# Layer 1's features split four chunks at once, tables first, four row buffers in layer 0's output projection, the last latent's k on VectorE, C's conversions moved

## The chip, the core and the metric

The kernel runs on one core of a Trainium2 chip. The metric is the device time of one execution in microseconds (us). The core has a tensor engine (PE, with the loading of its weights listed apart as PEld), a vector engine (VectorE, DVE), a scalar engine (ScalarE, ACT), a GpSimd engine (POOL) and a synchronising engine (SyncE, SP), which here issues nearly all DMAs, in its program's order. Each engine runs its own list of instructions in order and waits for the others by semaphores.

## The reference

Two layers of a transformer trunk work on 512 latent tokens and 128 context tokens of width 1024. Each layer is

```
m = silu(cond) @ w_mod + b_mod ; shift, scale, gate = split(m, 3)
h = rmsnorm(x, g) * (1 + scale) + shift
... = split(h @ w_in)                       # queries, keys, values, gates of two mixers
y = concat(attend1 * silu(gate1), attend2 * silu(gate2)) @ w_out
x = x + gate * y
```

with one conditioning vector for the latents and one for the context. Layer 0 has the mixers A (latent attention: 8 heads, queries and keys are made by an up-projection from a compressed row, normalised per head, rotated in their last 32 columns) and B (a neighbourhood attention). Layer 1 has C (grouped-query attention, 8 query heads on 2 key heads, rotary) and D (windowed attention with a sink logit). Latent queries read latent and cached context keys in one softmax; context tokens read context alone. The outputs are x of both groups and the layers' new cache rows. All is float32.

## The kernel before

The 640 tokens are five tiles of 128 (tiles 0 to 3 latents, tile 4 context). Every matrix product in float32 accuracy is done in three passes over a high part and a low part of both operands (`PASS`): ScalarE writes the high part as a rounded copy, and VectorE or GpSimd the low part as the difference. Weights come in 128x512 pieces in the order in which they are needed: `load_raw` (L165) fetches a piece on SP's queue into one of four buffers `raw`; `conv` takes the next piece, `split_w` splits it into a tile W or Wc (L171 the high part on ScalarE, L172 the low part on VectorE for odd pieces and on GpSimd for even ones) and then asks for another raw piece.

The program is written stage by stage, and a scheduler of the framework, which plays the program through with its own costs, sets the order on each engine. `after(key, f)` lets what f issues come no earlier than the instruction kept in `hold[key]`. Matmuls that nothing urgent needs (gates, the next mixer's inputs) are units of a list `filler`; `fill(ns)` emits units up to a budget between steps of attention, so that TensorE has work while a softmax runs.

The change touches three stages.

The end of A's up-projection: `e_up(t)` makes A's queries Aq and keys Ak of a tile. `e_q_end` multiplies Aq by its norm's factor on VectorE (L1046) and rotates it; for the context tile t = 4 that is one multiplication by the cosines, on GpSimd (L1050). `e_k` scales the key, on GpSimd (L1026 and the line after it). After the last tile eight pieces of layer 0's output weights are split. Then `a_prep(0)` transposes Ak and Aq (L660) for the first head. At the same time the modulation of layer 1 is computed: `matvec` (L223) multiplies columns of w_mod, loaded into `wm` (L215), of which there are two buffers.

Layer 0's output projection, with layer 1's features and its product C1 behind it: `out_proj` multiplies each tile's result by the gate (L1286, from PSUM to `otmp`) and adds it to the old row `xres` (L1287), which is loaded by DMA (L1255) into one buffer of the pool ldp for t = 0, 2, 4 and one of p for t = 1, 3. `l1_norm` stores the row and normalises it to `xn`. `l1_h` transposes xn four 128-column chunks at a time into one PSUM bank, and `h_evac` applies scale and shift per chunk: the high part (L282, ScalarE), the float32 value (L287 on VectorE for even chunks, L285 on ScalarE for odd ones) and the low part (L288, GpSimd for even, VectorE for odd). `l1_c1` (L302, from `tok_units`) multiplies by C1's weights; `cpost` behind it rotates with the tables that `tables` makes (L1324) from the row `orow` (L814).

The start of mixer C: pieces of GC (C's gate weights) are split, `fill` emits gate matmuls (L325), `k_prep` prepares the keys, `q_prep` transposes and splits the first two query heads (L634, L640), and the scores (L1515, L1517) begin.

## Time and profile before

Three runs took 821.66, 822.66 and 824.35 us, median 822.66 us. The profiled execution took 823.33 us, of which the recorded span is 821.6 us; 1.7 us lie outside the span.

| Engine | busy us | share of the span | instructions |
|---|---|---|---|
| PE | 756.0 | 92% | 4533 |
| PEld | 621.3 | 76% | 4533 |
| DVE | 590.8 | 72% | 1448 |
| ACT | 466.4 | 57% | 1189 |
| POOL | 245.3 | 30% | 303 |

The mean granted clock of TensorE is 0.981. The chain that ended last is put down to PE for 61%, to DVE for 17%, to ACT for 10% and to DMA for 5%. The DMA engines moved 85.19 MB, 104 GB/s over the span. A share is a mean over the whole span; which engine holds up which is seen in the waits of one stretch.

### The profile page before, as it was taken

The page shows a single profiled execution, that of the slowest core. Times are in us where ns is not written, and L with a number is a line of the kernel's source. Part 1 is how long each engine was busy: PE and PEld are TensorE (multiplying, and loading weights), DVE is VectorE, ACT ScalarE, POOL GpSimd, SP SyncE. Part 2 cuts the span into 40 slices and gives each one's busy share as a digit, 9 for nine tenths or more (in the row PEclk, how much of TensorE's full clock was granted, in tenths as well). Part 3 has the DMA queues.
Part 4 walks back from the last instruction along what each step waited for, and adds up shares of the span by engine and source line. Part 5 has one row for each costly group of instructions (what it writes and reads, how often), then busy time and mean ns, then how long its engine had stood idle before and what let it go on. Part 6 is the DMA issues. An engine that isn't in the chain of part 4 may idle for free.

```text
span 821.6 us, 13182 instructions
## 1 busy us (share of the span) xinstructions
PE 756.0 (92%) x4533; PEld 621.3 (76%) x4533; DVE 590.8 (72%) x1448; ACT 466.4 (57%) x1189; POOL 245.3 (30%) x303
## 2 busy tenths in 40 slices
PE   4797899999999979999999899799989998899998
PEld 3496898988989857777676677796858796876776
DVE  5466958686766778676676978678689876666855
ACT  6437575766656666454464757575445556745610
POOL 0465526262343550111031135103143420422210
PEclk9898999999999989999999999899999999999999
DMA  9957122211252077434475611203030110332144
GB/s 302 333 139 213 27 67 57 54 54 35 68 173 78 1 248 214 117 88 117 130 214 147 230 37 41 85 1 103 1 109 30 65 40 1 119 61 39 27 132 151
DMA packets 80436, 85.19 MB, mean 104 GB/s; under 512 B 7617, under 2 KB 64577, under 8 KB 80321
## 3 DMA queue, kind: packets, MB, share of 16 engines
q1 hardware_dynamic: 77488, 79.10, 31.7%
q0 software_dynamic: 2880, 5.24, 4.1%
q8 instruction: 36, 0.59, 0.3%
q14 instruction: 32, 0.25, 0.1%
HBM read 72.97 MB, written 13.98 MB: 106 GB/s over the span
## 4 chain that ended last, share of the span: by engine, by line
PE 61%; DVE 17%; ACT 10%; DMA 5%; issue 4%; POOL 2%; SPq 0%; DVEq 0%; ACTq 0%; POOLq 0%
PE ps_t L302 13%; PE ps_t L325 9%; PE ps_t L1130 6%; PE ps_t L1231 6%; PE ps_t L588 4%; PE ps_t L484 3%; PE ps_t L562 3%; PE ps_t L223 3%; PE ps_s L1203 2%; DVE W L172 2%; PE ps_s L772 2%; DVE P L417 2%; ACT W L171 2%; PE ps_t L461 1%; ACT P L428 1%
## 5 line engine op out<-in xcount | busy, mean ns | idle before, releaser
L302 PE MATMUL ps_t<-W,hT 128*128 128x384 f32 (+2 forms) x735 | 162.4, 368 | 8.7 <-DVE gB L337 3.0
L302 PEld LDWEIGHTS ps_t<-W,hT 128*128 128x128 f32 x735 | 131.6, 191 | 20.4 <-DVE gB L337 3.3
L325 PE MATMUL ps_t<-hT,W 128*128 128x320 f32 x768 | 125.5, 317 | 5.1 <-DVE W L172 1.9
L325 PEld LDWEIGHTS ps_t<-hT,W 128*128 128x128 f32 x768 | 116.3, 192 | 8.2 <-DVE W L172 2.2
L172 POOL TENSOR_TENSOR W<-raw,W 128x512 fp32r<-128x512 f32 (+1 forms) x54 | 73.3, 1362 | 92.3 <-ACT W L171 89.7
L171 ACT ACTIVATE W<-raw 128x512 fp32r<-128x512 f32 (+1 forms) x106 | 62.9, 620 | 24.1 <-DMA raw<-in_w_in_even 11.0
L1130 PE MATMUL ps_t<-W,ytp 128*128 128x512 f32 x240 | 62.9, 405 | 3.0 <-ACT PT L370 1.6
L370 ACT ACTIVATE PT<-ps_t 128x512 f32<-128x512 f32 (+2 forms) x80 | 42.2, 527 | 40.2 <-PE ps_t L562 22.5
L368 DVE COPY PT<-ps_t 128x512 f32<-128x512 f32 (+2 forms) x80 | 48.2, 604 | 23.0 <-PE ps_t L562 13.4
L533 ACT ACTIVATE P<-ps_s,m 128x640 f32<-128x640 f32 x64 | 50.6, 792 | 24.2 <-DVE m L532 15.9
L172 DVE TENSOR_TENSOR W<-raw,W 128x512 fp32r<-128x512 f32 (+1 forms) x52 | 50.5, 976 | 17.5 <-ACT W L171 17.2
L532 DVE TENSOR_REDUCE m<-ps_s 128x1 f32<-128x640 f32 x64 | 51.9, 817 | 9.4 <-PE ps_s L1517 4.9
L1130 PEld LDWEIGHTS ps_t<-W,ytp 128*128 128x128 f32 x240 | 43.2, 188 | 15.8 <-ACT PT L370 2.6
L428 ACT ACTIVATE P<-P,m 128x384 f32<-128x384 f32 (+3 forms) x64 | 42.3, 663 | 10.7 <-DVE m L417 10.4
L288 POOL TENSOR_TENSOR hT<-h,hT 128x128 fp32r<-128x128 f32 (+1 forms) x34 | 24.3, 722 | 80.0 <-ACT hT L282 36.4
L1231 PE MATMUL ps_t<-W,yt 128*128 128x512 f32 (+1 forms) x207 | 47.7, 384 | 0.0
L1231 PEld LDWEIGHTS ps_t<-W,yt 128*128 128x128 f32 x207 | 37.1, 188 | 8.6 <-DVE gb L368 0.4
L562 PE MATMUL ps_t<-ident,P 128*128 128x128 f32 x256 | 39.1, 277 | 2.2 <-DVE rt L115 1.0
L562 PEld LDWEIGHTS ps_t<-ident,P 128*128 128x128 f32 x256 | 29.8, 140 | 13.6 <-issue 5.6
L1139 POOL DMA_DIRECT2D part<-part x20 | 17.5, 873 | 73.6 <-DVE part L1136 73.6
L536 DVE TENSOR_SCALAR P<-P,den 128x640 f32<-128x640 f32 x64 | 37.3, 584 | 1.8
L461 PE MATMUL ps_t<-ident,P 128*128 128x128 f32 x224 | 31.7, 276 | 5.2 <-DVE PT L368 1.7
(307 smaller groups left out, 1632.9 us busy)
## 6 DMA issues: line engine op xcount, KB each, us to landing
wm<-in_w_mod SPq DMA_DIRECT2D x16, 1024.0 KB, 8.6
raw<-in_w_in_odd SPq DMA_DIRECT2D x40, 256.0 KB, 2.9
raw<-in_w_in_even SPq DMA_DIRECT2D x36, 256.0 KB, 3.6
wm<-in_w_mod SPq DMA_DIRECT2D x16, 512.0 KB, 5.2
part<-part POOLq DMA_DIRECT2D x20, 256.0 KB, 4.7
xres<-part SPq DMA_DIRECT2D x10, 512.0 KB, 4.1
raw<-in_w_out_even SPq DMA_DIRECT2D x16, 256.0 KB, 3.3
raw<-in_w_out_odd SPq DMA_DIRECT2D x16, 256.0 KB, 3.0
```

The source lines that it names most:

```text
L171: S.activation(out=dst_hi, in_=src, func=AF.Copy)
L172: (V if i % 2 else G).tensor_tensor(out=dst_lo, in0=src, in1=f32(dst_hi), op=OP.subtract)
L302: T.matmul(ps[:, 0:c1 - c0], lhsT=hT[:, k, x, 128 * t:128 * t + 128], rhs=W[c, k][:, y, c0:c1], start=(k == 0 and i == 0), stop=(k == 7 an ...
L325: T.matmul(ps[:, 0:320], lhsT=W[c, k][:, x, c0:c0 + 128], rhs=hT[:, k, y, 320 * hf:320 * hf + 320], start=(k == 0 and i == 0), stop=(k == ...
L368: V.tensor_copy(out, in_)
L370: S.activation(out=out, in_=in_, func=AF.Copy)
L428: S.activation(out=P[:, e, 0:n], in_=src[:, e, 0:n], func=AF.Exp, scale=-1.0, bias=m[:, e:e + 1], accum_out=den[:, e:e + 1])
L532: V.tensor_reduce(out=m, in_=s[:, :, 0:320], axis=AX.XY, op=OP.min)
L533: S.activation(out=P.rearrange("p (u n) -> p u n", u=2), in_=s[:, :, 0:320], func=AF.Exp, scale=-1.0, bias=m, accum_out=den)
L562: T.transpose(ps[:, 128 * b:128 * b + 128], P[:, 128 * b:128 * b + 128], ident)
L1130: T.matmul(ps, lhsT=yts[l, t][:, i, x, :], rhs=W["WO%d%d" % (l, hf), k][:, y, :], start=(i == 0 and j == 0), stop=(i == 3 and j == 2))
L1231: T.matmul(ps, lhsT=yt[:, i - i0, u, :], rhs=W["WO%d%d" % (l, hf), k][:, v, c0:c1], start=(i == 0 and j == 0), stop=(i == 3 and j == 2))
```

## The change

Six things are changed.

1. `conv`: the low part of every GC piece is made by VectorE, not by turns.
2. `h_evac4` replaces `h_evac` in layer 1. It takes four chunks at once: for the first four the scale and shift are two VectorE instructions over 512 columns with broadcast operands, for the other four ScalarE still does each chunk; then one ScalarE copy makes the high part and one subtraction over 512 columns the low part (GpSimd for the first four, VectorE for the others). The float32 value goes into xn itself.
3. For t = 4 `e_k` and the cosine multiplication of `e_q_end` run on VectorE, `e_k` first. The eight splits of output weights behind them are issued after the last high part of head 0's `a_prep`.
4. `out_proj` of layer 0 has one row buffer in ldp (t = 0 and 4) and three in p (t = 1 to 3); the loads of t = 1 to 3 are issued at the start.
5. `l1_start` makes the sink row and the tables of tiles 0 and 1 at once; before, they stood behind the normalisation of tile 1.
6. Four GC pieces are split after the features of tile 3 and four after those of tile 4 (before, all eight after the last). At the start of C the first `q_prep` stands ahead of the last 1900 ns of filler, and the tables of tile 3 behind it.

```diff
@@ -198,7 +198,7 @@
         w = ns * n
         t = wtile()
         r = raws.pop(i)
-        split_w(t[:, 0, 0:w], t[:, 1, 0:w], r[:, 0:w], i if odd is None else odd)
+        split_w(t[:, 0, 0:w], t[:, 1, 0:w], r[:, 0:w], (1 if c == "GC" else i) if odd is None else odd)
         W[c, k] = t
         if i < 4:
             after("raw", load_raw)
@@ -286,6 +286,22 @@
         else:
             V.tensor_scalar(out=t, in0=ps, scalar1=sc_, scalar2=sh_, op0=OP.mult, op1=OP.add)
         (V if mix and j % 2 or l == 0 and j == 7 else G).tensor_tensor(out=lo, in0=t, in1=f32(hi), op=OP.subtract)
+
+    def h_evac4(hT, l, q, n0, ps, h, v):
+
+        js = slice(4 * q, 4 * q + 4)
+        h3, ps3 = (z.rearrange("p (j n) -> p j n", j=4) for z in (h, ps))
+        if q:
+            for i in range(4):
+                j = 4 * q + i
+                S.activation(out=h3[:, i, :], in_=ps3[:, i, :], func=AF.Identity,
+                             scale=modS[:, l, j, v:v + 1], bias=modB[:, l, j, v:v + 1])
+        else:
+            V.tensor_tensor(out=h3, in0=ps3, in1=modS[:, l, js, v:v + 1].to_broadcast([128, 4, 128]), op=OP.mult)
+            V.tensor_tensor(out=h3, in0=h3, in1=modB[:, l, js, v:v + 1].to_broadcast([128, 4, 128]), op=OP.add)
+        hi = hT[:, js, 0, n0:n0 + 128]
+        hold["h"] = S.activation(out=hi, in_=h3, func=AF.Copy).ins
+        (V if q else G).tensor_tensor(out=hT[:, js, 1, n0:n0 + 128], in0=h3, in1=f32(hi), op=OP.subtract)
 
 
     def tok_units(hT, t, c, c0, c1, post, last):
@@ -624,7 +640,7 @@
             S.activation(out=hi, in_=src, func=AF.Copy)
             V.tensor_tensor(out=lo, in0=src, in1=f32(hi), op=OP.subtract)
         else:
-            S.activation(out=hi, in_=src, func=AF.Copy, scale=gain)
+            hold["hi"] = S.activation(out=hi, in_=src, func=AF.Copy, scale=gain).ins
             V.scalar_tensor_tensor(out=lo, in0=src, scalar=gain, in1=f32(hi), op0=OP.mult, op1=OP.subtract)
 
     def acopy(out, in_, gain=None):
@@ -1022,10 +1038,10 @@
         V.tensor_scalar(out=ss, in0=ss, scalar1=kss[:, t:t + 1], scalar2=None, op0=OP.add)
 
     def e_k(t, r):
-        rb = r[:, :, None]
-        G.tensor_tensor(out=Ak[:, t, :, 0:64], in0=Ak[:, t, :, 0:64], in1=rb.to_broadcast([128, 8, 64]), op=OP.mult)
-        hold["ak"] = G.tensor_tensor(out=Ak[:, t, :, 64:96], in0=rot[:, t, None, :].to_broadcast([128, 8, 32]),
-                                     in1=rb.to_broadcast([128, 8, 32]), op=OP.mult).ins
+        rb, eng = r[:, :, None], V if t == 4 else G
+        eng.tensor_tensor(out=Ak[:, t, :, 0:64], in0=Ak[:, t, :, 0:64], in1=rb.to_broadcast([128, 8, 64]), op=OP.mult)
+        eng.tensor_tensor(out=Ak[:, t, :, 64:96], in0=rot[:, t, None, :].to_broadcast([128, 8, 32]),
+                          in1=rb.to_broadcast([128, 8, 32]), op=OP.mult)
 
     def e_q(t, LT, ss):
         ps = ps_s()
@@ -1047,7 +1063,7 @@
         x = Aq[:, t, :, 64:96]
         cg = tabs[:, 0, t, None, :].to_broadcast([128, 8, 32])
         if t == 4:
-            G.tensor_tensor(out=x, in0=x, in1=cg, op=OP.mult)
+            V.tensor_tensor(out=x, in0=x, in1=cg, op=OP.mult)
             return
         m1 = ep.tile([128, 8, 32], F32, tag="qm1", name="qm1", bufs=1)
         m2 = ep.tile([128, 8, 32], F32, tag="qm2", name="qm2", bufs=1)
@@ -1068,8 +1084,11 @@
         e_q(t, LT, ss[:, 0:8])
         e_kv(t, lambda x: LT[:, x, 256:384], ss[:, 8:16])
         r = rstd(ep, ss, 16, 96, "e")
+        if t == 4:
+            e_k(t, r[:, 8:16])
         e_q_end(t, r[:, 0:8])
-        e_k(t, r[:, 8:16])
+        if t < 4:
+            e_k(t, r[:, 8:16])
 
     for i in range(3):
         filler.extend(gate_units(hT, "GA", 128 * i, new_gA, ep, False, 1))
@@ -1082,7 +1101,6 @@
     drain()
     tail = gate_units(hT, "GA", 384, new_gA, ep, False, 1)
     after("mm", lambda: emit(tail))
-    after("ak", lambda: after("act", lambda: [conv() for _ in range(8)]))
     ep.release()
     e0p.release()
     hp.release()
@@ -1191,6 +1209,8 @@
         hi_lo(ap, H[:, 512:768], L[:, 512:768], p3[0:96, 0:256], gmk[0:96])
         hi_lo(ap, H[:, 1280:1408], L[:, 1280:1408], p3[0:96, 256:384], gmq[0:96])
         AK[h] = (H, L)
+        if h == 0:
+            after("hi", lambda: [conv() for _ in range(8)])
 
     def a_score(h, t, s):
         t_ = AK[h]
@@ -1250,8 +1270,8 @@
             split_y(p, ysp[t], src, t, 1)
 
         def load(t):
-            q = ldp if l or t % 2 == 0 else p
-            xres[t] = q.tile([128, 1024], F32, tag="xres", name="xres", bufs=5 if l else 1)
+            q = ldp if l or t % 4 == 0 else p
+            xres[t] = q.tile([128, 1024], F32, tag="xres", name="xres", bufs=5 if l else 1 if q is ldp else 3)
             dma(out=xres[t], in_=parts[l][128 * t:128 * t + 128, :])
         load(0)
         if not gbs:
@@ -1259,17 +1279,16 @@
         split(0)
         load(1)
         split(1)
-        if l:
-            for t in range(2, 5):
-                load(t)
+        for t in range(2, 5 if l else 4):
+            load(t)
         start()
         for t in range(5):
             if l and 0 < t < 4:
                 split(t + 1)
             if not l and 0 <= t < 3:
                 split(t + 2)
-            if t < 3 and not l:
-                load(t + 2)
+            if t == 1 and not l:
+                load(4)
 
             steps = [(0, 0, 512), (1, 0, 512)] if not l or t < 4 else [(0, 0, 512), (1, 0, 256), (1, 256, 512)]
             for hf, c0, c1 in steps:
@@ -1416,6 +1435,9 @@
     def l1_start():
         dma(out=ropeO, in_=a["ropeO"])
         brow(orow, R_GQ, 520)
+        V.tensor_scalar(out=nsink, in0=orow[:, 512:520], scalar1=-1.0, scalar2=None, op0=OP.mult)
+        for i in range(2):
+            tables(i, V)
 
     def l1_half(t, cs, x):
         hf = cs.start // 512
@@ -1438,12 +1460,6 @@
             with tc.issue_after(hold["xn"]), tc.issue_after(hold["act"]):
                 for _ in range(4):
                     conv(1)
-        if t == 1:
-            def rows_():
-                V.tensor_scalar(out=nsink, in0=orow[:, 512:520], scalar1=-1.0, scalar2=None, op0=OP.mult)
-                for i in range(2):
-                    tables(i, V)
-            after("xn", rows_)
         pend.append((t, xn))
 
     def l1_h():
@@ -1454,8 +1470,7 @@
             for i in range(4):
                 j = 4 * q + i
                 T.transpose(ps[:, 128 * i:128 * i + 128], xn[:, 128 * j:128 * j + 128], ident)
-            for i in range(4):
-                h_evac(hT1, 1, 4 * q + i, 128 * t, 128, ps[:, 128 * i:128 * i + 128], op, v, True)
+            h_evac4(hT1, 1, q, 128 * t, ps, xn[:, 512 * q:512 * q + 512], v)
 
     pend = []
 
@@ -1471,9 +1486,10 @@
 
     out_proj(0, yAt, op, None, l1_start, l1_half, l1_done)
     l1_h()
+    after("h", lambda: [conv() for _ in range(4)])
     l1_c1(2)
     l1_h()
-    after("h", lambda: [conv() for _ in range(8)])
+    after("h", lambda: [conv() for _ in range(4)])
     l1_c1(3)
     l1_c1(4)
     ldp.release()
@@ -1495,14 +1511,16 @@
     wxc.release()
     for i in range(4):
         filler.extend(gate_units(hT1, "GC", 128 * i, new_g(gC), cp, i == 3))
-    tables(3)
     for t in range(5):
         filler.extend(tok_units(hT1, t, "C2", 0, 512, cpost(qc[1], kvD, 0, 3, ("new_swa_k", "new_swa_v")), t == 4))
     c2 = pool("c2", side="right")
     fill(CF0)
     KHc, KLc = k_prep(kvC, ctxk[:, 0, :], False)
-    fill(CF1)
+    fill(CF1 - 1900)
     Qc = {}
+    Qc[0], Qc[1] = q_prep(qc[0], 0)
+    tables(3)
+    fill(1900)
 
     def c_score(h, t, s):
         kvh, q = h // 4, Qc[h]
```

The scheduler's lists show what this moves. First VectorE at the end of A's up-projection, before (Aq and Ak are A's queries and keys, qm the halves of a rotation, rt and ry the norm's factor, gA the gate):

```order
L1058 TENSOR_TENSOR Aq<-qm_3124,qm_3125 128x8x32
L114 TENSOR_TENSOR rt<-ry 128x16
L115 TENSOR_TENSOR rt<-rt,rw 128x16
L172 TENSOR_TENSOR W<-raw,W 128x512
L116 SCALAR_TENSOR_TENSOR ry<-rt,ry 128x16
L1046 TENSOR_TENSOR Aq<-Aq,ry 128x768
L172 TENSOR_TENSOR W<-raw,W 128x512
L337 TENSOR_TENSOR gA<-ps_t,ge 128x320
```

and VectorE at the same place now:

```order
L1074 TENSOR_TENSOR Aq<-qm_3124,qm_3125 128x8x32
L114 TENSOR_TENSOR rt<-ry 128x16
L353 TENSOR_TENSOR gA<-ps_t,ge 128x320
L115 TENSOR_TENSOR rt<-rt,rw 128x16
L116 SCALAR_TENSOR_TENSOR ry<-rt,ry 128x16
L1042 TENSOR_TENSOR Ak<-Ak,ry 128x8x64
L1043 TENSOR_TENSOR Ak<-rot,ry 128x8x32
L1062 TENSOR_TENSOR Aq<-Aq,ry 128x768
L1066 TENSOR_TENSOR Aq<-Aq,tabs 128x8x32
```

Three multiplications have come over from GpSimd, and the splits of output weights (L172) have left this place.

SP's queue at the same time, before (raw are weight pieces, wm the columns of w_mod for layer 1):

```order
L165 DMA raw<-in_w_out_even 128x512 x4
L215 DMA wm<-in_w_mod 128x8x256
L165 DMA raw<-in_w_out_even 128x512
L215 DMA wm<-in_w_mod 128x8x256
L165 DMA raw<-in_w_out_even 128x512 x3
L215 DMA wm<-in_w_mod 128x8x256 x2
```

and SP's queue now:

```order
L215 DMA wm<-in_w_mod 128x8x256 x3
L165 DMA raw<-in_w_out_even 128x512 x4
L215 DMA wm<-in_w_mod 128x8x256
L165 DMA raw<-in_w_out_even 128x512 x4
```

Three loads of wm now stand ahead of the four raw pieces, and wm has two buffers, so the third waits for the first matvec, with the raw pieces behind it.

ScalarE in the features of layer 1, before (hT is the split feature, h its float32 value, kvC and sq belong to the product C1, ry to the norm of its heads):

```order
L632 ACTIVATE kvC<-ps_t 128x128
L1344 ACTIVATE sq<-ps_t 128x384
L282 ACTIVATE hT_4998<-ps_t,modB,modS 128x128 x3
L285 ACTIVATE h_5521<-ps_t,modB,modS 128x128
L104 ACTIVATE ry<-ss,epsc 128x6
L282 ACTIVATE hT_4998<-ps_t,modB,modS 128x128
L110 ACTIVATE ry<-ry 128x6
L285 ACTIVATE h_5584<-ps_t,modB,modS 128x128
```

and ScalarE there now:

```order
L648 ACTIVATE kvC<-ps_t 128x128
L1363 ACTIVATE sq<-ps_t 128x384
L297 ACTIVATE xn<-ps_t,modB,modS 128x128 x4
L303 ACTIVATE hT_4998<-xn 128x4x128
L171 ACTIVATE W<-raw 128x512 x4
L104 ACTIVATE ry<-ss,epsc 128x6
L303 ACTIVATE hT_4998<-xn 128x4x128
L110 ACTIVATE ry<-ry 128x6
```

The twelve chunk instructions of a tile have become four chunk instructions and two copies over 512 columns, and four splits of GC pieces (L171) stand among them.

## Rows read from the trace of the kernel before

**Rows 1.** Stretches: start:end, length, busy PE PEld DVE ACT POOL, PEclk, DMA share, GB/s.

```profile
318.00:437.00 119.00, 115.77 (x825) 82.65 (x824) 82.04 (x188) 55.61 (x131) 18.05 (x19) 1.00 0.56 145
...
468.00:475.00 7.00, 7.00 (x25) 5.61 (x24) 5.10 (x15) 4.80 (x14) 2.22 (x4) 0.76 0.41 150
482.00:507.00 25.00, 23.42 (x110) 18.97 (x109) 18.72 (x66) 17.79 (x52) 10.46 (x18) 1.00 0.09 29
...
519.00:531.00 12.00, 10.26 (x60) 9.97 (x59) 6.28 (x12) 6.65 (x17) 0.81 (x1) 0.84 0.27 80
531.00:597.00 66.00, 66.00 (x387) 55.31 (x386) 49.81 (x124) 40.14 (x102) 14.48 (x14) 1.00 0.11 33
```

**Rows 2.** Waits of PE, 289 to 303: releaser, total us, times, longest.

```profile
PE ps_t L660 <- POOL Aq L1050: 2.0, 1, 2.0
PE ps_t L660 <- DVE gA L337: 1.6, 1, 1.6
PE ps_t L223 <- DMA wm<-in_w_mod: 1.4, 1, 1.4
```

**Rows 3.** Waits of PE, 437 to 531, same columns.

```profile
PE ps_t L302 <- DVE otmp L1286: 2.3, 1, 2.3
PE ps_t L325 <- DVE W L172: 1.9, 1, 1.9
PE ps_s L1515 <- DVE Q L640: 1.7, 1, 1.7
PE ps_t L302 <- ACT h L285: 1.6, 2, 1.4
PE ps_t L325 <- POOL W L172: 1.2, 1, 1.2
PE ps_t L1456 <- DVE otmp L1286: 1.0, 1, 1.0
```

**Rows 4.** Timeline, VectorE and GpSimd, 289 to 295: start, duration, instruction, [idle before].

```profile
289.00 0.96 DVE L1046 TENSOR_TENSOR Aq<-Aq,ry 128x768 f32<-128x768 f32 x1
...
293.06 1.17 POOL L1050 TENSOR_TENSOR Aq<-Aq,tabs 128x256 f32<-128x256 f32 x1
```

**Rows 5.** The raw piece of 295.5, issued behind a load of wm.

```profile
L165 SPq DMA_DIRECT2D raw<-in_w_out_even x1: 327/327/327, 295.5 to 295.5; - x1
...
DMA to landing us min/median/max: 7.3/7.3/7.3
```

**Rows 6.** Timeline, ScalarE, 302 to 330: the exponentials of A's tile 3.

```profile
307.43 0.79 ACT L533 ACTIVATE P<-ps_s,m 128x640 f32<-128x640 f32 x1 [1.10 <-DVE m L532]
```

**Rows 7.** Timeline, PE, 435 to 560: like runs of matmuls.

```profile
468.67 6.31 PE L302 MATMUL ps_t<-Wc,hT 128*128 128x512 f32 x21
...
481.98 4.97 PE L302 MATMUL ps_t<-Wc,hT 128*128 128x512 f32 x21
...
519.19 6.54 PE L325 MATMUL ps_t<-hT,W 128*128 128x320 f32 x32
...
529.21 4.95 PE L325 MATMUL ps_t<-hT,W 128*128 128x320 f32 x32
```

**Rows 8.** Groups by shape, 437 to 531: line, operation, count, busy us, mean ns, idle.

```profile
L287 DVE TENSOR_SCALAR h<-ps_t,modS,modB 128x128 f32<-128x128 f32 x20 | 8.1, 407 | 1.6 <-POOL hT L288 0.7 <-ACT hT L282 0.4
L288 DVE TENSOR_TENSOR hT<-h,hT 128x128 fp32r<-128x128 f32 x20 | 7.0, 355 | 3.9 <-ACT h L285 3.9
L172 DVE TENSOR_TENSOR W<-raw,W 128x512 fp32r<-128x512 f32 x4 | 4.8, 1209 | 0.2
L172 DVE TENSOR_TENSOR Wc<-raw,Wc 128x512 fp32r<-128x512 f32 x7 | 4.5, 683 | 0.0
L1324 DVE TENSOR_TENSOR tab<-ropeO,orow 128x320 f32<-128x320 f32 x4 | 1.7, 479 | 0.0
L282 ACT ACTIVATE hT<-ps_t,modB,modS 128x128 fp32r<-128x128 f32 x40 | 17.8, 459 | 8.7 <-DVE h L287 4.5 <-PE ps_t L1456 4.0
```

**Rows 9.** The row `orow`, issued on SP's queue at 437.0.

```profile
DMA to landing us min/median/max: 4.4/4.4/4.4
```

## The prediction

> **What bounds the kernel now.** I read three views in turn: the windows by stage, the waits of PE inside the stages the change touches, and the rows of the instructions those waits name. [rows 1] says that PE is the engine to follow: mixer A keeps it busy 115.77 of 119 us and the middle of C 66.00 of 66, at a granted clock of 1.00, while VectorE has 82.04 and 49.81 us there. What runs earlier ahead of such a stretch therefore moves all behind it and is kept to the end. Gaps lie between: ahead of A, in the output projection with layer 1's features and C1, and ahead of C. [rows 2, 3] list what PE waited for in them. Two waits end on instructions that change engine: 2.0 us for GpSimd's cosine product (L1050) and 1.2 us for a split on GpSimd. The others end on VectorE or ScalarE work that is replaced or moved.
>
> **The start of A.** Before, VectorE multiplies Aq at 289.00 for 0.96 us, and GpSimd starts the cosines only at 293.06, behind the key, for 1.17 us, so Aq is ready at 294.23 [rows 4]. With the change VectorE has the key's 512 and 256 columns, Aq's 768 and the cosines' 256. At 0.96 us for 768 (an estimate by columns) these are 0.64 + 0.32 + 0.96 + 0.32 = 2.24 us, ready at 289.00 + 2.24 = 291.24, 3.0 us earlier. PE's wait of 2.0 us [rows 2] began near 292.3, so it goes whole. What is late next is the gate product, whose 1.6 us wait [rows 2] may go too, since the splits that stood ahead of it on VectorE leave, or the loads. Three loads of wm now stand ahead of the raw pieces on SP's queue, the third until the first matvec has read its buffer. If PE gets there at about 297.5 (an estimate: the 302.2 at which its 1.4 us wait for wm ended [rows 2], less that wait and the other waits here, 302.2 - 1.4 - 3.6 = 297.2), the raw pieces go out then, and with the 7.3 us that one behind a wm took [rows 5] the first lands at 304.8. Behind the splits on ScalarE stand exponentials of A; the one of tile 3 ran at 307.43 [rows 6] and would come near 305.4 with 2.0 us gained, so the splits have little to spare, and A's scores wait for whoever comes late. Bounds: nothing gained (the raw pieces take it back; more than that is rival 4) to 5.0 (all three waits of the stretch). I take the row nearest to the edit, **2.0**.
>
> **Output projection, features, C1.** PE waited 2.3 and 1.0 us for VectorE's gating product otmp and 1.6 us for a feature's float32 value on ScalarE [rows 3]: 4.9 us. VectorE loses the tables from this place (4 x 0.479 = 1.9 us [rows 8], now at the start, where it idled) and need not wait for a row: all three loads go out first. A tile's features cost ScalarE before 8 x 0.459 plus 4 like them, 5.5 us [rows 8], and afterwards 4 x 0.459 and two copies of 512 columns, each between 0.459 and 4 x 0.459 us (I take 0.63, near the 0.683 of VectorE's 512 columns), 3.1 us. VectorE paid 4 x 0.407 + 4 x 0.355 = 3.0 us [rows 8], and pays three instructions of 512 columns at 0.683, 2.0 us. GpSimd has one instruction of 512 columns for four of 128. The latency of a tile's first half grows (two products, a copy and a subtraction in a row, near 3 us), but PE has the product of an earlier tile then. A PSUM bank is also free after two reads on VectorE, and not after eight chunk reads on two engines. After the waits the granted clock was 0.76 in 468 to 475, between its two levels, and 1.00 in 482 to 507 [rows 1]: 21 like matmuls took 6.31 us there and 4.97 here [rows 7]. Without the gaps that 1.3 goes as well. Together **6.2**; bounds 0, if VectorE is as late as before (a loss is excluded here but for the tables and splits below, since each engine has less to do per tile), to 6.2.
>
> **The start of C.** PE's gate matmuls waited 1.9 us for a split on VectorE and 1.2 us for one on GpSimd [rows 3], since all eight splits came after the last features. Four of the eight are done earlier, and none is left to GpSimd: 3.1 us. The clock of the gate run behind them was low in part, 0.84 over the stretch [rows 1]: 32 like matmuls took 6.54 us, and 4.95 later [rows 7], 1.6 more. Together **4.7**. The 1.7 us for Q [rows 3] I count as kept: q_prep stands ahead of 24 more gate matmuls, but its transposes need PSUM banks that k_prep's readers still hold. Bounds of the stage: 0 to 6.4.
>
> **What the new order costs.** The tables and the sink row now wait on VectorE for orow, which landed 4.4 us after 437.0 [rows 9], at 441.4, and the first gating products queue behind them. Four splits more stand among the features. The tables alone are 1.9 us; a part is hidden by the PE work already queued, so I take 1.0 of it, with bounds 0 and 2.0. The loads of three rows at once fall into DMA time that is half idle (share 0.41 in 468 to 475 [rows 1]); without that cover the addition behind a gating product would wait for its row, up to the 4.4 us in which orow landed [rows 9].
>
> **Sum.** 2.0 + 6.2 + 4.7 - 1.0 = 11.9 us. The profiled execution took 823.33 us, so 811.4; it stood 0.67 above the median of the three runs, so the forecast is **810.8 us**. Its own range: with A at 5.0 and nothing for the tables, 806.8; with A at 0 and half of the second term, 815.9. I set 805.5 to 815.
>
> **Rivals.**
>
> (1) VectorE becomes the bound of C1. It was busy 18.72 of 25 us from 482 to 507 [rows 1], more than half full in every part of the stage, and gets four splits of 0.683 to 1.209 us each [rows 8], 2.7 to 4.8 us, against a saving of 1.0 us a tile. At 21 to 23 of 25 the gating products are late as before: the 4.9 us of the three waits stay, 815.7. The split rows speak for it: the same 512-column subtraction takes 0.683 us at one time and 1.209 at another, when GpSimd splits too [rows 8]. Against it: GpSimd now does fewer instructions there. The Trainium skill ("SBUF — State Buffer", section "Who interferes with whom") has a rule for this pair: a VectorE instruction with two inputs in SBUF contends with a GpSimd instruction that reads SBUF, because its second input comes over the shared read interface. The trace agrees with 1.209 against 0.683 us; by that rule the new subtractions of 512 columns on GpSimd would lengthen VectorE's additions and splits beside them.
>
> (2) Nothing comes of it: the waits change names and PE starts the same work at the same time, because the loop of row, normalisation, features and product has another slowest link, such as the square and store of the row. 822, within 0.3% (2.5 us, about what a measurement of this kernel tells from no change, so 820.2 to 825.1). Against it: the waits have six different releasers in three places, and a stretch with PE at 66.00 of 66 [rows 1] lies behind and carries what is gained.
>
> (3) All of it is gained: A 5.0, Q's 1.7 and no cost of the tables: 17.6 us, 805.1. For it: the new order takes each named releaser out of its place. Against it: in [rows 2] three releasers follow one another within 14 us, and the time of one that goes is in part time that another then shows.
>
> (4) Slower, through SP's queue at the start of A. The raw pieces stand behind three loads of wm, whose third waits for PE; ScalarE takes splits of those pieces ahead of exponentials. If the four pieces land one after another, 4 x 7.3 = 29.2 us [rows 5], the last lands at 297.5 + 29.2 = 326.7, and the exponential due at 305.4 waits 21.3 us. With the other two stages gaining 9.9, 823.3 + 21.3 - 9.9 is 834.7, or 834.1 by the median. It decides once ScalarE stands over 9.9 us longer than before, and counts as slower from 12.4. Against it: pieces issued together land together, and one was held up by a wm by some microseconds, not by four. The Trainium skill ("DMA: Bandwidth & Descriptors", section "Two DMAs through the same engine are not ordered") says that within one queue of one DMA engine descriptors start in order. That fits the 7.3 us of a piece behind a wm, and by it the four share one wait and not four.
>
> **How the numbers follow.** Forecast 0.58; rival 1 0.20; rival 2 0.09; rival 3 0.07; rival 4 0.06. Faster by more than 0.3% are the forecast, rivals 1 and 3: 0.85; no change 0.09; slower 0.06. The range 804.0 to 818.5 holds the forecast, rival 1 and rival 3, and at its upper end A at 0 with half of the second and third terms less 1.0 (4.5 us, 818.2). It leaves out rivals 2 and 4, 0.15.
>
> **What would show it.** In the changed kernel's trace PE's wait for Aq ahead of A is gone, and the first exponentials come about 2 us earlier; if ScalarE idles there for raw pieces, the start of A was misjudged. PE's waits for otmp and h in the output projection are under 1 us together, and the runs of 21 and 32 matmuls take near 5 us everywhere; if waits for VectorE remain, rival 1. The gate matmuls ahead of C's scores wait for no split; a wait for Q of about 1.7 us remains. The stretches of A and of the middle of C keep their lengths. The prediction is wrong if they grow, or if a wait of several microseconds for a DMA appears.

## The result and the profile after

The changed kernel took 811.41 us in the median of four runs (809.77 to 813.47), before 823.27 in the same rounds: a ratio of 0.9865, 95% interval 0.9835 to 0.9896. In a later set of rounds it took 812.27, ratio 0.9874 (0.9850 to 0.9898). The forecast was 810.8, with a range of 804.0 to 818.5.

The profiled execution took 809.77 us, span 808.0. I follow the 13.6 us of difference in span by four points of PE's timeline: A's first transposes of Ak, the first matmul of the output projection, the first scores of C, and a run of 24 C2 matmuls in the middle of C. A length is the difference of two starts (to the end of C1, of a start and an end).

| stretch | before | after | less |
|---|---|---|---|
| start to A's transposes | 289.27 | 286.27 | 3.00 |
| A, to the output projection | 150.11 | 147.73 | 2.38 |
| output projection to end of C1 | 68.37 | 64.05 | 4.32 |
| output projection to C's first scores | 88.53 | 80.55 | 7.98 |
| output projection to the C2 run | 153.96 | 146.60 | 7.36 |
| C2 run to the end | 228.26 | 227.40 | 0.86 |

The first row needs care: no edit is aimed at that part. In the thirteen profiles of changed kernels A's transposes start between 286.27 and 293.14 us, and the kernel before lies between, so its 3.0 us are not put down to the change. The last row's 0.9 is left out too: over the same profiles (but the run with less fill) that stretch takes 227.4 to 229.1 us. What can be the change's in this pair is 2.4 + 7.4 us, some 9.8.

PE's waits at the start of A, changed kernel, 286 to 303 (releaser, us in total, times, longest), where [rows 2] had 2.0, 1.6 and 1.4. P are the exponentials of a softmax, AH and AL the high and low part of A's queries and keys:

```profile
PE ps_s L1223 <- ACT P L549: 1.7, 1, 1.7
PE ps_t L676 <- DVE Aq L1066: 0.8, 1, 0.8
PE ps_s L1223 <- ACT AH L643: 0.4, 1, 0.4
```

The waits for the gate product and for wm are gone, the one for Aq has shrunk from 2.0 to 0.8, and with two new ones 2.9 us of waits stand there. The rows behind them, VectorE's timeline and then ScalarE's, changed kernel (start, duration, instruction):

```profile
285.79 0.69 DVE L1042 TENSOR_TENSOR Ak<-Ak,ry 128x512 f32<-128x512 f32 x1
286.40 0.42 DVE L1043 TENSOR_TENSOR Ak<-rot,ry 128x256 f32<-128x256 f32 x1
286.74 0.95 DVE L1062 TENSOR_TENSOR Aq<-Aq,ry 128x768 f32<-128x768 f32 x1
287.72 0.43 DVE L1066 TENSOR_TENSOR Aq<-Aq,tabs 128x256 f32<-128x256 f32 x1
```

```profile
291.74 2.20 ACT L171 ACTIVATE W<-raw 128x512 fp32r<-128x512 f32 x4
...
294.18 0.80 ACT L549 ACTIVATE P<-ps_s,m 128x640 f32<-128x640 f32 x1
```

VectorE's four instructions (three of them came from GpSimd) end 2.4 us after their start (forecast 2.24), and PE waits 0.8 us for Aq and not 2.0. The 1.7 us are A's first exponential behind four splits of output weights. The splits found their pieces in place; the pieces issued behind the loads of wm landed in 3.9 to 5.3 us, and from 286 to 345 ScalarE waited for none of them.

PE's waits in the output projection, the features, C1 and up to C's scores, changed kernel, 434 to 531, against the six rows of [rows 3] (KH and KL are the high and low part of C's keys, nss a row's sum of squares, g a gate):

```profile
PE ps_t L676 <- DVE KL L654: 1.0, 1, 1.0
PE ps_t L1251 <- DVE otmp L1305: 0.9, 1, 0.9
PE ps_t L1472 <- DVE nss L1456: 0.6, 1, 0.6
PE ps_t L341 <- DVE KL L654: 0.3, 1, 0.3
PE ps_t L676 <- DVE g L353: 0.2, 1, 0.2
```

3.0 us are left where those six rows had 9.7. No wait for h, a split or Q remains. The run of [rows 7] that took 6.31 us takes 4.97:

```profile
461.25 4.97 PE L318 MATMUL ps_t<-Wc,hT 128*128 128x512 f32 x21
```

In the middle of C, which was to stay as it was, something is given back. The windows of the changed kernel (columns as in [rows 1]) and the longest of PE's waits from 531 to 600:

```profile
472.00:497.00 25.00, 24.95 (x125) 20.73 (x124) 22.81 (x54) 17.09 (x45) 8.74 (x9) 1.00 0.33 104
...
515.00:531.00 16.00, 16.00 (x117) 15.97 (x116) 10.67 (x24) 10.60 (x27) 0.61 (x1) 1.00 0.01 2
531.00:583.50 52.50, 49.87 (x262) 38.84 (x261) 39.26 (x99) 28.59 (x72) 12.94 (x13) 0.97 0.13 41
```

```profile
PE ps_t L596 <- DVE PTp L384: 2.1, 1, 2.1
```

C1 (first row) has PE at 24.95 of 25 us, where [rows 1] had 23.42. In the last row PE is no longer busy throughout, and its clock is 0.97, not 1.00. PE's own timeline there, then VectorE's and GpSimd's:

```profile
541.10 0.46 PE L596 MATMUL ps_t<-PTp,kvC 128*64 128x128 f32 x4 [2.08 <-DVE PTp L384]
541.49 1.12 PE L578 MATMUL ps_t<-ident,P 128*128 128x128 f32 x4
542.26 5.13 PE L318 MATMUL ps_t<-W,hT 128*128 128x512 f32 x16
```

```profile
535.94 0.55 DVE L552 TENSOR_SCALAR P<-P,den 128x640 f32<-128x640 f32 x1
...
536.81 1.78 DVE L172 TENSOR_TENSOR W<-raw,W 128x512 fp32r<-128x512 f32 x1
...
538.58 0.67 DVE L172 TENSOR_TENSOR W<-raw,W 128x512 fp32r<-128x512 f32 x1
539.17 1.55 DVE L552 TENSOR_SCALAR P<-P,den 128x640 f32<-128x640 f32 x1
540.64 0.41 DVE L384 COPY PTp<-ps_t 128x256 f32<-128x256 f32 x1
```

```profile
536.74 1.29 POOL L172 TENSOR_TENSOR W<-raw,W 128x512 fp32r<-128x512 f32 x1 [9.61 <-ACT W L171]
538.55 1.81 POOL L172 TENSOR_TENSOR W<-raw,W 128x512 fp32r<-128x512 f32 x1 [0.52 <-ACT W L171]
```

The copy PTp (the transposed weights of the context queries) stands on VectorE behind two splits of C2 weights and a rescaling. The rescaling takes 1.55 us beside GpSimd's second split, and 0.55 with GpSimd idle. VectorE's first split begins 0.07 us behind GpSimd's first and takes 1.78. In the second pair, which begin within 0.03 us of each other, VectorE's takes 0.67 and GpSimd's is the longer one, 1.81 in place of 1.29. The Trainium skill ("SBUF — State Buffer", section "Who interferes with whom") names such pairs: some VectorE instructions hold or need ports that GpSimd shares, and whoever comes second waits. The trace agrees in that one of each pair is long and the other is not (1.78 and 1.29, 0.67 and 1.81); 0.03 us do not tell who came first in the second.

Meanwhile PE has no gate matmul left: by the lists 96 stand ahead of C's first scores, where 72 did. After the wait 16 matmuls take 5.13 us; at the rate of the 21 of one shape above (4.97) they would take 3.8. So in this execution the wait and the clock cost 2.1 + 1.3 = 3.4 us. The clock's part is not fixed. Four of the runs below (old splits, old rows, old tables, chunks alone) have the same wait of 2.1 us and kept a clock of 1.00; they took 64.55 us from the first scores to the C2 run, where the changed kernel took 66.05 at 0.97.

### The profile page after: what moved, and what is told of

Read it like the earlier page. It is cut to its first block, busy times and chain, and to the rows that moved or that the text cites. A ratio compares the mean times of both kernels' runs of the same rounds, so it can differ in the third digit from the quotient of the medians.

```text
span 808.0 us, 13091 instructions
## 1 busy us (share of the span) xinstructions
PE 750.4 (93%) x4533; PEld 617.2 (76%) x4533; DVE 592.5 (73%) x1430; ACT 456.0 (56%) x1159; POOL 234.3 (29%) x281
## 4 chain that ended last, share of the span: by engine, by line
PE 55%; DVE 21%; ACT 11%; issue 5%; DMA 5%; POOL 3%; SPq 0%; DVEq 0%; ACTq 0%; POOLq 0%
PE ps_t L318 11%; PE ps_t L341 7%; PE ps_t L1148 6%; PE ps_t L1251 5%; PE ps_t L604 4%; PE ps_t L500 3%; PE ps_t L578 3%; DVE W L172 3%; PE ps_t L223 3%; PE ps_s L1223 2%; ACT W L171 2%; DVE P L433 2%; ACT P L444 2%; DMA raw<-in_w_in_even 1%; DVE m L548 1%
## 5 line engine op out<-in xcount | busy, mean ns | idle before, releaser
L341 PE MATMUL ps_t<-hT,W 128*128 128x320 f32 x768 | 122.1, 312 | 1.6 <-DVE KL L654 0.7
L341 PEld LDWEIGHTS ps_t<-hT,W 128*128 128x128 f32 x768 | 114.0, 188 | 3.6 <-PE ps_t L676 1.0
L172 POOL TENSOR_TENSOR W<-raw,W 128x512 fp32r<-128x512 f32 (+1 forms) x50 | 68.6, 1376 | 98.1 <-ACT W L171 97.6
L171 ACT ACTIVATE W<-raw 128x512 fp32r<-128x512 f32 (+1 forms) x106 | 62.6, 620 | 17.0 <-DMA raw<-in_w_in_even 10.6
L172 DVE TENSOR_TENSOR W<-raw,W 128x512 fp32r<-128x512 f32 (+1 forms) x56 | 52.9, 955 | 16.8 <-ACT W L171 16.8
L549 ACT ACTIVATE P<-ps_s,m 128x640 f32<-128x640 f32 x64 | 50.7, 794 | 24.2 <-DVE m L548 13.6
L548 DVE TENSOR_REDUCE m<-ps_s 128x1 f32<-128x640 f32 x64 | 51.8, 815 | 11.9 <-PE ps_s L1535 9.0
L578 PEld LDWEIGHTS ps_t<-ident,P 128*128 128x128 f32 x256 | 30.5, 143 | 12.8 <-issue 5.6
L477 PEld LDWEIGHTS ps_t<-ident,P 128*128 128x128 f32 x224 | 25.8, 141 | 8.0 <-ACT PT L386 1.6
```

The costliest lines, as they stand in the source:

```text
L171: S.activation(out=dst_hi, in_=src, func=AF.Copy)
L172: (V if i % 2 else G).tensor_tensor(out=dst_lo, in0=src, in1=f32(dst_hi), op=OP.subtract)
L341: T.matmul(ps[:, 0:320], lhsT=W[c, k][:, x, c0:c0 + 128], rhs=hT[:, k, y, 320 * hf:320 * hf + 320], start=(k == 0 and i == 0), stop=(k == ...
L477: T.transpose(ps[:, 128 * b:128 * b + 128], P[:, e, 128 * b:128 * b + 128], ident)
L548: V.tensor_reduce(out=m, in_=s[:, :, 0:320], axis=AX.XY, op=OP.min)
L549: S.activation(out=P.rearrange("p (u n) -> p u n", u=2), in_=s[:, :, 0:320], func=AF.Exp, scale=-1.0, bias=m, accum_out=den)
```

## The experiments

All start from the changed kernel unless it is said otherwise, and are given as ratios to the kernel before in the same rounds. Lengths in us, from one profile each:

| run | ratio, 95% | A | to C1 end | to scores | to C2 run |
|---|---|---|---|---|---|
| before | 1 | 150.1 | 68.4 | 88.5 | 154.0 |
| changed | 0.9865 (0.9835 to 0.9896) | 147.7 | 64.1 | 80.6 | 146.6 |
| changed again | 0.9874 (0.9850 to 0.9898) | 146.8 | 63.8 | 80.3 | 146.4 |
| old latent | 0.9879 (0.9856 to 0.9901) | 148.8 | 63.7 | 80.3 | 146.3 |
| old splits | 0.9910 (0.9888 to 0.9932) | 151.8 | 63.7 | 80.2 | 144.8 |
| old chunks | 0.9917 (0.9886 to 0.9949) | 147.7 | 68.6 | 87.4 | 150.8 |
| old rows | 0.9879 (0.9846 to 0.9912) | 147.7 | 63.4 | 81.5 | 146.0 |
| old tables | 0.9856 (0.9826 to 0.9887) | 147.7 | 63.0 | 79.5 | 144.1 |
| old GC splits | 0.9875 (0.9844 to 0.9906) | 147.7 | 64.9 | 82.3 | 148.4 |
| chunks alone | 0.9920 (0.9890 to 0.9949) | 149.2 | 64.8 | 82.4 | 146.9 |
| C2 on GpSimd | 0.9801 (0.9780 to 0.9822) | 147.0 | 63.4 | 81.4 | 143.1 |
| less fill | 0.9862 (0.9841 to 0.9882) | 149.2 | 63.7 | 80.2 | - |
| C2 on GpSimd, old tables | 0.9836 (0.9809 to 0.9863) | 146.8 | 63.0 | 81.0 | 142.7 |
| C2 on GpSimd, late splits | 0.9851 (0.9824 to 0.9878) | 148.3 | 63.7 | 80.2 | 141.9 |

**The start of A, both edits undone.**

```diff
-        rb, eng = r[:, :, None], V if t == 4 else G
...
+        rb = r[:, :, None]
...
-            V.tensor_tensor(out=x, in0=x, in1=cg, op=OP.mult)
+            G.tensor_tensor(out=x, in0=x, in1=cg, op=OP.mult)
...
+    after("ak", lambda: after("act", lambda: [conv() for _ in range(8)]))
...
-        if h == 0:
-            after("hi", lambda: [conv() for _ in range(8)])
```

> The changed kernel with the third edit undone (the last latent's key and cosines on GpSimd again, the eight splits of output weights right behind them). Theory: the stretch from the last gate run of the up-projection (48 like matmuls) to the first matmul of the output projection, 157.2 us before and 154.8 in the changed kernel, grows back to about 157.2, PE waits some 2 us for Aq on GpSimd's L-line of the cosines, and the time is about 2.4 us above the changed kernel's 811.4, so 813.8. Rival, that the stretch is shorter by chance or for another reason: it stays near 154.8 and the time near 811.4.

814.92 us. PE's waits, 286 to 304:

```profile
PE ps_t L676 <- POOL Aq L1066: 2.0, 1, 2.0
PE ps_t L676 <- DVE gA L353: 1.5, 1, 1.5
```

The waits of [rows 2] are back, but for wm's. The stretch grew by 1.1 to 2.0 us (against 147.7 and 146.8), less than the 2.4 expected, and the interval of the ratio covers the changed kernel's two ratios. At the start of A the waits are as the theory says, but over the whole of A PE stands idle for 8.3 us here, for 8.4 in the changed kernel and for 9.4 before. So it is not shown that the wait for Aq cost any time. What differs is the granted clock (the third figure from the end, where 1.00 is 2.4 GHz and 0.50 is 1.2). The first 30 us of A in the kernel before, the changed kernel, this run and the run with less fill below, whose code for A is that of the changed kernel:

```profile
289.27:319.27 30.00, 24.28 (x183) 19.25 (x184) 25.67 (x56) 19.86 (x47) 10.65 (x9) 0.89 0.75 242
...
286.27:316.27 30.00, 25.29 (x207) 20.07 (x208) 28.19 (x63) 22.16 (x52) 8.09 (x6) 0.94 0.56 180
...
289.60:319.60 30.00, 25.41 (x197) 20.09 (x195) 26.48 (x59) 20.34 (x49) 10.60 (x9) 0.89 0.78 246
...
287.82:317.82 30.00, 25.33 (x194) 19.45 (x192) 27.30 (x61) 21.32 (x51) 8.14 (x6) 0.89 0.56 176
```

**Only the place of the splits undone** (the last three lines of the diff above, with `hold["ak"]` on VectorE's instruction).

> The changed kernel with only the place of the eight splits as before; key and cosines of the last latent stay on VectorE. Theory that the engine brings the gain (the step as predicted, 2.0 us from GpSimd's wait): the same stretch stays at 154.8 to 155.4. Rival that the place of the splits and of their loads on SP's queue brings it: the stretch is 156.5 to 157.5, with waits of PE for the gate product (1.6) or for wm (1.4) as before.

816.40 us. PE's waits, 286 to 304, VectorE's timeline and GpSimd's:

```profile
PE ps_t L676 <- DVE gA L353: 6.1, 2, 3.8
PE ps_s L1222 <- ACT AH L643: 1.2, 1, 1.2
```

```profile
287.11 1.19 DVE L116 SCALAR_TENSOR_TENSOR ry<-rt,ry 128x16 f32<-128x16 f32 x1
288.34 0.69 DVE L1042 TENSOR_TENSOR Ak<-Ak,ry 128x512 f32<-128x512 f32 x1
288.95 1.48 DVE L1043 TENSOR_TENSOR Ak<-rot,ry 128x256 f32<-128x256 f32 x1
...
291.22 1.28 DVE L172 TENSOR_TENSOR W<-raw,W 128x512 fp32r<-128x512 f32 x2
```

```profile
286.98 3.17 POOL L172 TENSOR_TENSOR W<-raw,W 128x512 fp32r<-128x512 f32 x2 [0.65 <-ACT W L171]
```

Neither guess: the stretch of the expectation is 158.9 us, and A became longer than before, 151.8. With the splits in their old place VectorE has its three new products and the splits at once, and the product of 256 columns, begun beside GpSimd's two splits, takes 1.48 us in place of 0.42. The engine's change does not pay with the splits in the way. The other half, the splits moved and the products left on GpSimd, was not run.

**C2's low parts on GpSimd.**

```diff
-        split_w(t[:, 0, 0:w], t[:, 1, 0:w], r[:, 0:w], (1 if c == "GC" else i) if odd is None else odd)
+        split_w(t[:, 0, 0:w], t[:, 1, 0:w], r[:, 0:w], (1 if c == "GC" else 0 if c == "C2" else i) if odd is None else odd)
```

> The changed kernel with the low parts of all C2 pieces on GpSimd. In the changed kernel PE waits 2.1 us for the copy PTp in mixer C, behind two splits and a rescaling of 1.55 us on VectorE, and 16 matmuls behind it take 5.13 us in place of about 3.9. Theory that the two splits on VectorE cause the wait: it falls to under 0.7 us and the matmuls behind it run at full clock, 2 to 3 us less, about 808.5 to 809.5. Rival that VectorE's instructions beside GpSimd's splits are slow anyway (1.55 for a rescaling that takes 0.55 alone): the wait keeps 1 us or more, the C2 products then wait for GpSimd's splits, 811 to 813.

807.59 us (806.77 to 809.04). The wait and the matmuls behind it:

```profile
540.34 0.44 PE L596 MATMUL ps_t<-PTp,kvC 128*64 128x128 f32 x4 [0.40 <-DVE PTp L384]
...
541.12 1.89 PE L318 MATMUL ps_t<-W,hT 128*128 128x512 f32 x7
```

0.40 us are left of 2.08, seven matmuls take 1.89 (16 took 5.13), and the stretch to the C2 run is 3.5 us shorter. From the first scores to the C2 run it takes 61.65 us at a clock of 1.00, 2.9 less than the 64.55 of the runs with the wait at that clock. The splits on VectorE were the cause. VectorE's rescalings still take 1.0 to 1.15 us there, GpSimd splitting beside them, but that no longer decides. This version beats both kernels.

**Less fill ahead of C.**

```diff
     tables(3)
-    fill(1900)
```

> The changed kernel without the last fill(1900) ahead of mixer C's first head, so that 24 gate matmuls stand behind the product with PTp, where the changed kernel has none left. Theory that PE lacks independent work there: the wait of 2.1 us for PTp goes or is under 0.7, time 808.5 to 810. Rival that the work is only taken from another place: a wait of about the same size turns up ahead of the first scores or later in C, 811 to 812.5.

812.41 us. The wait for PTp falls to 0.3, but from 435 to 660 PE waits elsewhere, where the changed kernel has 1.3 for P and none for Pp:

```profile
PE ps_s L1532 <- ACT P L549: 2.3, 3, 1.1
...
PE ps_s L1532 <- ACT Pp L565: 1.0, 1, 1.0
```

The time is within the rival's range and the waits are elsewhere in C, so the rival holds: the gate matmuls were only taken from another place.

**The chunk split undone.**

```diff
-            h_evac4(hT1, 1, q, 128 * t, ps, xn[:, 512 * q:512 * q + 512], v)
+            for i in range(4):
+                h_evac(hT1, 1, 4 * q + i, 128 * t, 128, ps[:, 128 * i:128 * i + 128], op, v, True)
```

> The changed kernel with layer 1's features split chunk by chunk as before. Theory that the chunk instructions made the features late (1.6 us wait for h) and held PSUM banks and VectorE: the stretch from the first matmul of the output projection to the end of C1, 68.4 us before and 63.4 to 64.1 in the changed kernel and its variants, grows by 2 to 4 us, to 66 to 68; PE's wait for the copy PTp in mixer C is absent, since the lists there are those of before; time 812 to 815. Rival that the features are off the path: the stretch stays under 64.7.

815.91 us; the stretch to the end of C1 is as long as before, 68.6, but it holds 24 gate matmuls, where the changed kernel has 9 and the one before 2. At 4.95 / 32 each [rows 7] it is 2.2 us longer than the changed kernel's at equal work, and 3.2 shorter than before. PE's waits, 435 to 600:

```profile
PE ps_t L676 <- DVE kvC L1375: 6.7, 1, 6.7
PE ps_t L318 <- ACT h L285: 1.6, 2, 1.4
PE ps_t L1251 <- DVE otmp L1305: 1.0, 1, 1.0
```

The wait for h is back in its full 1.6. The row kvC of C1 is late by 6.7; that VectorE now has all of GC's splits and the chunks too is the likely reason, which no run tests. The wait for PTp is absent, as expected.

**Row buffers undone** (one buffer in each pool, `load(t + 2)` in the loop).

> The changed kernel with layer 0's rows in one buffer of each pool and loaded in the loop, as before. Theory of the prediction (the loads were hidden but for half a microsecond): the stretch to the end of C1 grows by 0 to 0.7 us, time within 1 us of the changed kernel's. Rival that late rows made the gating products late (2.3 and 1.0 us of waits for otmp before): it grows by 2 to 3.5 us.

812.94 us, 63.4 to the end of C1: no longer than with three buffers. The edit brings nothing there. Behind it PE waits 1.9 us for kvC, where the changed kernel has no such wait, and the scores come 0.9 to 1.2 us later, at a clock of 0.91 between the end of C1 and the scores; whether the buffers do that stays open.

**Tables undone** (`after("xn", rows_)` at tile 1).

> The changed kernel with the sink row and the tables of tiles 0 and 1 behind the normalisation of tile 1 again. Theory of the prediction (1.9 us of VectorE out of the busy part, 1.0 of them paid at the start): the stretch to the end of C1 grows by about 1 us, with a wait for otmp of 1 to 2 us near the first features. Rival that VectorE had room there: no change, or 0.5 us less since nothing waits for orow.

812.28 us, and 63.0 to the end of C1, 0.8 to 1.0 us less than the changed kernel. The rival holds: VectorE had room for the tables later. Early, VectorE stands 2.0 us for orow, and PE waits 0.9 us for a gating product, a wait that is absent here. To the C2 run this profile is 2.3 to 2.5 us shorter, but 1.5 of them are the clock in C, 1.00 here and 0.97 there, with the same wait for PTp.

**GC's splits undone** (parity, and eight splits after the last features).

> The changed kernel with GC's pieces split by turns on VectorE and GpSimd and all eight after the last features, as before. Theory of the prediction: PE's gate matmuls ahead of C's scores wait for splits again (1.9 and 1.2 us before), with a slow clock behind, so the stretch from the output projection's first matmul to C's first scores, 80.2 to 81.4 us now with as many gate matmuls ahead, grows by 3 to 4.7 us. Rival that the earlier end of the features alone did it: it grows by less than 1.5 us.

814.01 us. The scores come 1.7 to 2.0 us later, with as many gate matmuls ahead; expected were 3 to 4.7. The waits for splits are 0.4 and not 3.1, which fits features that end earlier; KH of the keys is late by 2.2 instead. Between theory and rival.

**The chunk split alone, on the kernel before** (`h_evac4` added, and the call above in `l1_h`).

> The kernel before with the four-chunk split of the features as its only edit. Theory, from the run that undid it: it alone brings the second term; the stretch to the end of C1 falls from 68.4 to 63 to 65 us, and to the C2 run from 154.0 to 148 to 150, while the start of A stays at 150; time 817.5 to 819.5. Rival that it needs the row buffers or the tables to work: the stretch to the end of C1 stays above 66.5 and the time above 820.5.

814.99 us (ratio 0.9920), faster than expected; 64.8 to the end of C1 with 13 gate matmuls, 5.2 us less than before at equal work, and 146.9 to the C2 run, 7.0 us less than before. Alone, one edit has nearly all that the change gains behind A. PE's wait of 2.1 us for PTp is there too: what is given back in C comes with the same edit. A, whose code is that of before, took 149.2 at a clock of 0.89.

**Two tries for more**, both on C2 on GpSimd: with the tables in their old place, and with the eight splits after the second head's `a_prep`.

> The changed kernel with C2's low parts on GpSimd and with the tables behind tile 1's normalisation as before. Theory that both edits add up: the stretch from the output projection to the run of 24 C2 matmuls, 146.6 us in the changed kernel, 143.1 with C2 on GpSimd, 144.1 with the old tables, is 141 to 142.5, time 0.5 to 2 us under that of C2 on GpSimd alone (807.6), so 805.5 to 807. Rival that the old tables' gain was a clock that stayed high by chance: 143 to 144, 807.5 to 808.5.

> The changed kernel with C2's low parts on GpSimd and the eight output-weight splits after the second head's last high part in place of the first head's. In the changed kernel four of them (2.2 us) stand on ScalarE ahead of A's first exponentials, and PE waits 1.7 us for one. Theory that these splits cause that wait: with the two first exponentials ahead of or among them the wait falls under 0.8 us and the stretch from the first transposes of A to the output projection, 147.0 to 147.7 us, is 145.8 to 146.8; time about 1 us under 807.6. Rival that the wait only moves to the next exponential or to late output weights: 147 to 148.5.

808.63 and 810.51 us; neither is better than 807.59, by the ratios too. The old tables shorten the stretch to the C2 run by 0.4, to 142.7, and the time not at all: nearer to the rival, and the clock is what it named. With later splits PE's waits for P are 2.3 us in three places and 1.5 for a rescaling: the wait only moved, and A took 148.3.

**The changed kernel again.**

> The changed kernel once more, in the same rounds as the three above, for comparison. The theory that the start of the program, which no edit touches, differs from run to run expects A's first transposes at another time than the 286.3 us of its first profile (before 289.3), with the stretches behind as before: 147.0 to 147.8 for A, 63.4 to 64.1 to the end of C1, 2.1 us of wait for PTp; time 811 to 812.5. The rival, that the change moved that point, expects 286.3 within 0.5 us.

812.27 us. A's transposes start at 287.92, with A 146.8 us, the end of C1 and the PTp wait (2.1) as in the first profile of the changed kernel: 1.7 of the 3.0 us ahead of A are gone without any edit, and the rival, 286.3 within 0.5, does not hold. The clock in the first 30 us of A was 1.00 here and 0.94 there.

## Why the prediction was right

The forecast of 810.8 stands against 811.41 and 812.27. By its own steps:

- **Start of A, 2.0.** The size fits, the mechanism is not shown. A is 2.4 shorter in the pair of profiles. Of the row taken, GpSimd's 2.0 us, 0.8 stayed; the gate product's 1.6 and wm's 1.4 went too, and 1.7 came back as an exponential behind splits on ScalarE. That place was named, but its price was put on the landing of raw pieces, and it was the splits' own 2.2 us. Over the whole of A PE idles 1.0 us less than before, but with both edits undone it is 1.1 less too. The length goes with the granted clock, for which the sum has no term. At 0.89 in its first 30 us A took 148.8, 149.2 and 150.1 with the old code and 149.2 with the new (less fill); the new took 147.7 at 0.94, five times, and 146.8 to 147.0 at 1.00, three times. The low clock stands in all three profiles of the old code and in one of nine of the new, so the edits may act through the clock; that stays open.
- **Output projection, features, C1, 6.2 less 1.0.** The stretch is 4.3 shorter and holds seven more gate matmuls (9, not 2), 1.1 us at 4.95 / 32 each [rows 7]: 5.4 against 5.2. But the working credited tables and rows with a part. With the rows or the tables undone the stretch is no longer, and the chunk split alone brings 5.2 of the 5.4. Without it the other edits together still bring 3.2, so the edits overlap, and no share can be given to each. The 1.0 for early tables was right: 0.8 to 1.0.
- **Start of C, 4.7.** From the end of C1 to the scores 20.2 us became 16.5, with 17 more gate matmuls, another 2.6: 6.3 at equal work. That is the 4.7 and also the 1.7 for Q that I had counted as kept, so this term was mis-sized. Its cause was not mainly the four earlier splits (1.7 to 2.0 us, by the run with GC's splits undone) but features that ended sooner: the chunk split alone took the same part to 17.6 us with 13 more gate matmuls, 4.6 at equal work.
- **"The stretches of A and of the middle of C keep their lengths."** This step failed in C. From the first scores to the C2 run the changed kernel took 66.0 us and before 65.4, although 24 gate matmuls (3.7 us) had already been done: 4.3 us given back, 3.4 of them at the copy behind VectorE's splits. With C2 on GpSimd that stretch is 4.4 us shorter, or 2.9 against runs at the same clock. So the terms read 2.4 + 5.4 + 6.3 - 4.3 = 9.8 us where 11.9 were forecast. That the forecast hit is in part luck: one term too small stood against a loss that was put at nothing, and the first term's gain came with a clock that the sum did not have.
- **Rivals.** Rival 1 did not come true in C1, where VectorE was busy 22.81 of 25 us and PE 24.95. VectorE held PE up in the middle of C instead, busy 39.26 of 52.5 us, by two splits that stood ahead of one copy. SP's queue did no harm: the pieces behind wm landed in 3.9 to 5.3 us.
- **The median.** 9.8 us are seen in the pair of profiles behind A's start, 10.7 and 11.9 in the two pairs of medians. Single runs of the changed kernel scatter by 3.7 and 5.5 us in the two sets of rounds, so that difference stays open.

## What to carry to other kernels

Filler matmuls that run earlier are missing where they ran before: when a gap ahead of a stage is closed, look for the next wait inside the stage, at the point where the filler now ends. A busy engine that splits weights ahead of a short copy in the critical order is the first suspect, and moving that work to the idle engine is one line. Where several edits go into one place, undo them one by one, and run the strongest alone as well: here one of six brought nearly all behind the start of A by itself, yet undoing it took back only a part, and one cost a little. Compare stretches at equal work, and look at the granted clock of each before a difference of 1 to 2 us is put down to an edit.

## What the hardware showed beside it

- Program parts that are the same took different times from run to run: A's first transposes began at 286.27 to 293.14 us. In the latest of these the granted clock was 0.89 from 40 to 100 us, in the earliest 0.94.
- The same code with the same waits ran at different clocks: A took 146.8 us at a granted clock of 1.00 in its first 30 us, 147.7 at 0.94 and 149.2 at 0.89, and with the same 2.1 us of wait for PTp the stretch behind C's first scores took 64.55 us at 1.00 and 66.05 at 0.97.
- Some of VectorE's instructions grew beside GpSimd's splits: a product of 128x256 from 0.42 to 1.48 us, a rescaling of 128x640 from 0.55 to 1.55.
- GpSimd's one subtraction of 512 columns took 1.44 us in the mean, where four of 128 had taken 2.0.
